# Sharing the block moves of every tile pair between two engines, with fewer and larger transfers in a new order

## Chip, cores and metric

One core of one Trainium2 chip. The metric is the device time of one execution in microseconds (us); the span of a profile is from the first to the last instruction and is some 1.7 us shorter.

## The reference

```python
batch, m, k, n = 16, 512, 1024, 768
# x (16, 512, 1024), weight (1024, 768), add_value (16, 512, 768), all float32; scale = 0.1
return (scale * np.matmul(x, weight) + add_value).astype(np.float32)
```

The 8192 rows of x are 64 tiles of 128 rows. 87 MB move through the core: x 33.6, weight 3.1, add_value 25.2, result 25.2.

## The kernel before

All transfers are issued by SyncE, in the order of a list: x, weight (w), add (a), out (o), each with first tile and number of tiles. Sixteen slots hold x tiles, thirty-two hold add tiles, in which the result is also formed. The weight is staged in add slots 24 to 31.

```python
STREAM = [
    ("x", 0, 3), ("w", 0, 2), ("w", 2, 2), ("w", 4, 2), ("x", 3, 1), ("w", 6, 2),
    ("a", 0, 3), ("x", 4, 4), ("a", 3, 1), ("a", 4, 4), ("x", 8, 4), ("x", 12, 4),
    ("x", 16, 4), ("a", 8, 8), ("x", 20, 4), ("x", 24, 8), ("o", 0, 8), ("a", 16, 8),
    ("x", 32, 8), ("a", 24, 8), ("a", 32, 8), ("x", 40, 8), ("o", 8, 8), ("x", 48, 8),
    # ... cut
    ("a", 56, 8), ("o", 40, 8), ("o", 48, 8), ("o", 56, 4), ("o", 60, 1), ("o", 61, 1),
    ("o", 62, 1), ("l", 63, 1), ("r", 63, 1),          # l, r: the two column parts of one tile
]
X_SLOTS = 16; A_SLOTS = 32; XB_BUFS = 3
MOVED_ACT = [14, 18, 22, ..., 58]      # pairs moved by ScalarE
MOVED_POOL = [16, 20, 24, ..., 56]     # pairs moved by GpSimd
```

TensorE needs x transposed and in bf16. Tiles 0 to 13 and 60 to 63 are cast and transposed by TensorE. The pairs of tiles between are transposed without it: sixteen copies of 32 partitions each cast the pair and rearrange its blocks (the moves), then VectorE turns 32x32 blocks in one instruction. A pair of x slots is free for the next load once it has been moved.

```python
va_pool = tc.tile_pool(name="va_pool", bufs=2)     # pairs moved by ScalarE
vp_pool = tc.tile_pool(name="vp_pool", bufs=2)     # pairs moved by GpSimd

def move_pair(t0, a):                               # called for a = 0..3
    act = t0 in MOVED_ACT
    ...                                             # a == 0: a buffer from va_pool or vp_pool
    for b in range(4):
        move = nc.scalar.copy if act else nc.gpsimd.tensor_copy
        move(moved[t0][32*b:32*b+32, :, a, :], src[32*a:32*a+32, :, b, :])

def step():                                         # one tile
    for j in range(KJ):
        if j == KJ // 2:
            if t + 1 not in in_pair: transpose(t + 1)
            cast_to(min(t + AHEAD, done["x"] - 1))
            for a in range(4):
                if in_pair.get(t + 8 - a) == t + 8 - a: move_pair(t + 8 - a, a)
        product(t, j, BOTH)                         # 512 and 256 columns, bf16
    finish(t, BOTH[0], 0, N)                        # VectorE: scale * product + add, in place
    if in_pair.get(t + 4) == t + 4: turn_moved(t + 4)
```

VectorE runs in program order, so the turn of pair t + 4 comes after the finish of tile t, which may have to wait for its add tile.

Of the kernel before, what the change touches and what calls it, by code (L numbers as in the profile page):

```python
# [9 lines left out]


STREAM = [
    ("x", 0, 3), ("w", 0, 2), ("w", 2, 2), ("w", 4, 2), ("x", 3, 1), ("w", 6, 2),
    ("a", 0, 3), ("x", 4, 4), ("a", 3, 1), ("a", 4, 4), ("x", 8, 4), ("x", 12, 4),
    ("x", 16, 4), ("a", 8, 8), ("x", 20, 4), ("x", 24, 8), ("o", 0, 8), ("a", 16, 8),
    ("x", 32, 8), ("a", 24, 8), ("a", 32, 8), ("x", 40, 8), ("o", 8, 8), ("x", 48, 8),
    ("a", 40, 8), ("o", 16, 8), ("x", 56, 8), ("a", 48, 8), ("o", 24, 8), ("o", 32, 8),
    ("a", 56, 8), ("o", 40, 8), ("o", 48, 8), ("o", 56, 4), ("o", 60, 1), ("o", 61, 1),
    ("o", 62, 1), ("l", 63, 1), ("r", 63, 1),
]  # L20

X_SLOTS = 16
# [3 lines left out]
EARLY = 3  # L26



MOVED_ACT = [14, 18, 22, 26, 30, 34, 38, 42, 46, 50, 54, 58]  # L30
MOVED_POOL = [16, 20, 24, 28, 32, 36, 40, 44, 48, 52, 56]


@with_exitstack
def kernel(
# [8 lines left out]
    nc = tc.nc  # L44
    P = 128
    bf16 = mybir.dt.bfloat16
# [9 lines left out]
    KC = K // (2 * P)  # L56
# [8 lines left out]
    def rows(view, s, n):  # L65
        assert s // G == (s + n - 1) // G
        return view[:, s // G, s % G:s % G + n, :]


    w_v = weight.rearrange("(c p r) n -> p c r n", p=P, r=2)  # L70

    const = ctx.enter_context(tc.tile_pool(name="const", bufs=1))
    xb_pool = ctx.enter_context(tc.tile_pool(name="xb_pool", bufs=XB_BUFS))
    xt_pool = ctx.enter_context(tc.tile_pool(name="xt_pool", bufs=3))
    va_pool = ctx.enter_context(tc.tile_pool(name="va_pool", bufs=2))
    vp_pool = ctx.enter_context(tc.tile_pool(name="vp_pool", bufs=2))
    tp_pool = ctx.enter_context(
        tc.tile_pool(name="tp_pool", bufs=2, space=bass.MemoryType.PSUM))
    mm_pool = ctx.enter_context(
# [6 lines left out]
    ao = const.tile([P, A_SLOTS, N], fp32, name="ao")  # L86
    w_bf = const.tile([P, KJ, N], bf16, name="w_bf")

    xb_tiles, xt_tiles, mm_tiles, done = {}, {}, {}, {"cast": 0, "step": 0, "x": 0}
    in_pair = {t0 + i: t0 for t0 in MOVED_ACT + MOVED_POOL for i in range(2)}  # L90
    moved, cast_pairs = {}, set()

    def load_w(j, n):

        s = A_SLOTS - KJ + j
        if n == 1:
            nc.sync.dma_start(ao[:, s, :], w_v[:, j // 2, j % 2, :])
        else:
            nc.sync.dma_start(ao[:, s:s + 2, :], w_v[:, j // 2, :, :])  # L99
        for i in range(n):  # L100
            nc.vector.tensor_copy(w_bf[:, j + i, :], ao[:, s + i, :])  # L101

    def move_pair(t0, a):


        act = t0 in MOVED_ACT
        if a == 0:
            if act:
                va = va_pool.tile([P, 2 * KC, 4, 64], bf16, tag="va")
            else:  # L110
                va = vp_pool.tile([P, 2 * KC, 4, 64], bf16, tag="vp")
            moved[t0] = va
        k = t0 % X_SLOTS
        assert k + 1 < X_SLOTS
        src = xs[:, k:k + 2, :].rearrange("p i (c b k) -> p (i c) b k", b=4, k=64)
        for b in range(4):
            move = nc.scalar.copy if act else nc.gpsimd.tensor_copy
            move(moved[t0][32 * b:32 * b + 32, :, a, :], src[32 * a:32 * a + 32, :, b, :])  # L118
        if a == 3:
            cast_pairs.add(t0)  # L120

    def turn_moved(t0):
        xt = xt_pool.tile([P, 2, KC, P], fp32, tag="xt")
        for i in range(2):
            xt_tiles[t0 + i] = xt[:, i, :, :]
        nc.vector.transpose(  # L126
            xt.rearrange("p i c m -> p (i c m)"),
            moved.pop(t0).bitcast(fp32).rearrange("p c a k -> p (c a k)"))

    def cast_to(t):  # L130
        while done["cast"] <= t:
            i = done["cast"]
            if i in in_pair:
                assert in_pair[i] in cast_pairs
                done["cast"] += 1
                continue
            if len(xb_tiles) == XB_BUFS:
                break
            xb = xb_pool.tile([P, K], bf16, tag="xb")
            src = xs[:, i % X_SLOTS, :]  # L140
            if i < EARLY:
                nc.vector.tensor_copy(xb[:, 0:K // 2], src[:, 0:K // 2])  # L142
                other = nc.gpsimd.tensor_copy if i else nc.scalar.copy
                other(xb[:, K // 2:K], src[:, K // 2:K])  # L144
            else:
                nc.gpsimd.tensor_copy(xb, src)  # L146
            xb_tiles[i] = xb
            done["cast"] += 1

    def transpose(t, pieces=1):  # L150
        cast_to(t)

        pairs = xb_tiles.pop(t).bitcast(fp32)
        tp = tp_pool.tile([P, KC, P], fp32, tag="tp")
        for c in range(KC):
            nc.tensor.transpose(tp[:, c, :], pairs[:, c * P:(c + 1) * P], identity)  # L156
        if t % 2 == 0:
            xt = xt_pool.tile([P, 2, KC, P], fp32, tag="xt")
            for i in range(2):
                xt_tiles[t + i] = xt[:, i, :, :]  # L160
        q = KC // pieces
        evacuate = nc.scalar.copy if t <= EARLY or t > LAST_PAIR else nc.vector.tensor_copy
        for c in range(0, KC, q):
            evacuate(  # L164
                xt_tiles[t][:, c:c + q, :].bitcast(bf16), tp[:, c:c + q, :].bitcast(bf16))
# [5 lines left out]
    def product(t, j, cols):  # L171
        if (t, cols[0]) not in mm_tiles:
            mm = mm_pool.tile([P, 1024], fp32, tag="mm")
            for part in cols:
                mm_tiles[t, part] = mm
        for n0, n1 in cols:
            nc.tensor.matmul(  # L177
                mm_tiles[t, cols[0]][:, n0:n1], lhs(t, j), w_bf[:, j, n0:n1],
                start=(j == 0), stop=(j == KJ - 1))
# [3 lines left out]
    def finish(t, part, n0, n1):  # L183
        a = ao[:, t % A_SLOTS, n0:n1]
        nc.vector.scalar_tensor_tensor(  # L185
            a, mm_tiles[t, part][:, n0:n1], float(scale), a,
            op0=mybir.AluOpType.mult, op1=mybir.AluOpType.add)
# [27 lines left out]
                        op0=mybir.AluOpType.mult)  # L215
            done["step"] = EARLY

    LAST_PAIR = max(in_pair)
    EARLY_AT = A_SLOTS - KJ - EARLY

    def step():
        t = done["step"]
        if t < T - 1:
            for j in range(KJ):
                if j == KJ // 2:
                    if t + 1 not in in_pair:
                        transpose(t + 1)
                    cast_to(min(t + AHEAD, done["x"] - 1))
                    for a in range(4):
                        if in_pair.get(t + 8 - a) == t + 8 - a:  # L230
                            move_pair(t + 8 - a, a)
                product(t, j, BOTH)
            finish(t, BOTH[0], 0, N)
            if in_pair.get(t + 4) == t + 4:
                turn_moved(t + 4)
        else:
            for cols in BOTH:
                for j in range(KJ):
                    product(t, j, [cols])
                finish(t, cols, *cols)  # L240
        done["step"] += 1

    def added(t):
        assert done["step"] >= EARLY
        nc.vector.tensor_add(  # L245
            ao[:, t, :], ao[:, EARLY_AT + t, :], ao[:, t, :])

    for op, s, n in STREAM:
        last = s + n - 1
        if op == "w":  # L250
            load_w(s, n)
            head(op, s, n)
        elif op == "x":
            if last >= X_SLOTS:
                while done["cast"] <= last - X_SLOTS:
                    step()
            k = s % X_SLOTS
            nc.sync.dma_start(xs[:, k:k + n, :], rows(x_v, s, n))  # L258
            done["x"] = s + n
            if last < EARLY:  # L260
                head(op, s, n)
        elif op == "a":
            k = s % A_SLOTS
            nc.sync.dma_start(ao[:, k:k + n, :], rows(add_v, s, n))  # L264
            for t in range(s, min(s + n, EARLY)):
                added(t)
        else:
            while done["step"] <= last:
                step()
            k = s % A_SLOTS  # L270
            n0, n1 = {"o": (0, N), "l": (0, CUT), "r": (CUT, N)}[op]
            nc.sync.dma_start(rows(out_v, s, n)[:, :, n0:n1], ao[:, k:k + n, n0:n1])  # L272
# [35 lines left out]
```

## Time and profile before

| | before |
|---|---|
| time, median (lowest to highest), us | 210.12 (210.09 to 210.5) |
| data queue: packets, share of 16 engines' span | 5616, 98.2% |
| busy: TensorE, VectorE, ScalarE, GpSimd | 87%, 49%, 62%, 60% |

The share of the queue, the time for which the 16 DMA engines are busy with its packets, is what to read first. Here are the moves, from the costliest groups of the kernel before (partitions x elements, count, then busy us and mean ns of one, then idle time before them):

```profile
L118 ACT CAST va<-xs 32x512 bf16<-32x512 f32 x192 | 118.2, 616 | 28.8 <-DMA xs<-in_x_dram 19.1
L118 POOL CAST va<-xs 32x512 bf16<-32x512 f32 x176 | 106.8, 607 | 15.9 <-DVE xt L126 6.2
```

A pair is sixteen of them on one engine, about 10 us, with the two engines working on different pairs side by side.

### The profile page before, as it was taken

What the parts mean: (1) busy time and instruction counts of PE and PEld (TensorE: products, weight loads), DVE (VectorE), ACT (ScalarE), POOL (GpSimd) and SP (SyncE); (2) the same over time, 40 slices, a digit from 0 to 9 for tenths busy, and PEclk for the clock granted to TensorE, in tenths of its full rate; (3) what the DMA queues carried; (4) which work ended last, traced back from release to release, by engine and by line L of the source; (5) the groups of instructions that cost most, each with busy time, mean ns of one, the idle gap of its engine ahead of it and who ended that gap; (6) DMA issues with size and microseconds to landing.
All of it is one profiled execution on the core that took longest, in us unless ns stands there. A gap on an engine that the chain in (4) does not pass through costs nothing.

```text
span 208.5 us, 2886 instructions
## 1 busy us (share of the span) xinstructions
PE 181.6 (87%) x1096; PEld 110.7 (53%) x1096; DVE 101.3 (49%) x111; ACT 129.0 (62%) x206; POOL 124.3 (60%) x199
## 2 busy tenths in 40 slices
PE   0599399980899997999999999999999999989960
PEld 0455256650466664566666666666666666656630
DVE  0536535511466514855655555555553685233330
ACT  2423000499959798599999999999999900003210
POOL 1310524379898980999998899999999960001000
PEclk9999889996589999999999999999999999999997
DMA  6999999999999999999999999999999999999995
GB/s 236 415 428 440 413 429 434 421 450 406 454 418 448 407 429 462 404 443 420 442 434 413 461 418 424 420 429 437 421 434 424 432 439 424 429 418 439 429 394 214
DMA packets 5629, 87.21 MB, mean 418 GB/s; under 512 B 624, under 2 KB 752, under 8 KB 2032
## 3 DMA queue, kind: packets, MB, share of 16 engines
q1 hardware_dynamic: 5616, 87.03, 98.2%
q8 instruction: 8, 0.13, 0.3%
q14 instruction: 5, 0.04, 0.0%
HBM read 61.87 MB, written 25.17 MB: 417 GB/s over the span
## 4 chain that ended last, share of the span: by engine, by line
DMA 75%; ACT 9%; PE 7%; DVE 3%; SPq 1%; issue 1%; DVEq 0%
DMA out_dram<-ao 35%; DMA ao<-in_add_value_dram 22%; DMA xs<-in_x_dram 13%; ACT va L118 9%; PE mm L177 6%; DMA ao<-in_weight_dram 5%; DVE ao L185 2%; DVE xt L126 1%; PE tp L156 1%; SPq L258 1%; SPq L99 0%; SPq L264 0%; SPq L272 0%; DVEq L185 0%
## 5 line engine op out<-in xcount | busy, mean ns | idle before, releaser
L177 PE MATMUL mm<-w_bf,xt 128*128 128x256 bf16 (+1 forms) x1024 | 173.8, 331 | 8.8 <-DVE xt L164 6.6
L177 PEld LDWEIGHTS <-xt 128*128 128x128 bf16 x1024 | 101.3, 99 | 76.9 <-DVE xt L164 7.0
L118 ACT CAST va<-xs 32x512 bf16<-32x512 f32 x192 | 118.2, 616 | 28.8 <-DMA xs<-in_x_dram 19.1
L118 POOL CAST va<-xs 32x512 bf16<-32x512 f32 x176 | 106.8, 607 | 15.9 <-DVE xt L126 6.2
L185 DVE SCALAR_TENSOR_TENSOR ao<-mm,ao 128x768 f32<-128x768 f32 (+2 forms) x62 | 58.1, 942 | 78.1 <-PE mm L177 49.1
L146 POOL CAST xb<-xs 128x1024 bf16<-128x1024 f32 x15 | 15.2, 1040 | 43.4 <-PE tp L156 22.5
L164 ACT COPY xt<-tp 128x512 bf16<-128x512 bf16 (+1 forms) x11 | 8.2, 785 | 35.3 <-PE tp L156 35.3
L126 DVE STREAM_TRANSPOSE xt<-va 128x1024 f32<-128x1024 f32 x23 | 28.4, 1234 | 0.0
L156 PE MATMUL tp<-identity,xb 128*128 128x128 f32 x72 | 12.9, 314 | 11.2 <-DVE xb L142 7.4
L156 PEld LDWEIGHTS tp<-identity,xb 128*128 128x128 f32 x72 | 9.8, 161 | 13.7 <-issue 7.6
L164 DVE COPY xt<-tp 128x1024 bf16<-128x1024 bf16 x10 | 6.9, 686 | 10.1 <-PE tp L156 10.1
L101 DVE CAST w_bf<-ao 128x768 bf16<-128x768 f32 x8 | 4.1, 556 | 3.8 <-DMA ao<-in_weight_dram 3.8
L142 DVE CAST xb<-xs 128x512 bf16<-128x512 f32 x3 | 1.9, 696 | 6.8 <-DMA xs<-in_x_dram 6.8
L144 POOL CAST xb<-xs 128x512 bf16<-128x512 f32 x2 | 1.6, 834 | 5.5 <-DMA xs<-in_x_dram 5.5
L144 ACT CAST xb<-xs 128x512 bf16<-128x512 f32 x1 | 0.6, 618 | 4.8 <-DMA xs<-in_x_dram 4.8
L213 DVE TENSOR_SCALAR ao<-mm 128x768 f32<-128x768 f32 x2 | 1.8, 952 | 1.9 <-PE mm L177 1.9
L245 DVE TENSOR_TENSOR ao<-ao 128x768 f32<-128x768 f32 x3 | 2.7, 951 | 0.0
L144 ACT ACT_TABLE_LOAD x1 | 1.3, 1283 | 0.7 <-PEq L289 0.7
L210 ACT ACTIVATE ao<-mm 128x768 f32<-128x768 f32 x1 | 0.8, 817 | 0.0
masks.py:197 POOL MEMSET identity<- 128x128 f32 x1 | 0.2, 204 | 0.3 <-POOLq L289 0.3
masks.py:199 POOL TENSOR_SCALAR_AFFINE_SELECT identity<-identity 128x128 f32<-128x128 f32 x1 | 0.3, 292 | 0.1
L289 POOL MEMSET const-float32-0.0<- 128x1 f32 x1 | 0.1, 98 | 0.2 <-issue 0.2
(3 smaller groups left out, 0.3 us busy)
## 6 DMA issues: line engine op xcount, KB each, us to landing
ao<-in_add_value_dram SPq DMA_DIRECT2D x7, 3072.0 KB, 26.1
out_dram<-ao SPq DMA_DIRECT2D x7, 3072.0 KB, 23.9
xs<-in_x_dram SPq DMA_DIRECT2D x5, 4096.0 KB, 18.8
xs<-in_x_dram SPq DMA_DIRECT2D x5, 2048.0 KB, 26.6
ao<-in_weight_dram SPq DMA_DIRECT2D x4, 768.0 KB, 9.6
xs<-in_x_dram SPq DMA_DIRECT2D x1, 1536.0 KB, 6.1
ao<-in_add_value_dram SPq DMA_DIRECT2D x1, 1536.0 KB, 19.3
out_dram<-ao SPq DMA_DIRECT2D x1, 1536.0 KB, 12.9
```

What stands on the lines that cost most here:

```text
L101: nc.vector.tensor_copy(w_bf[:, j + i, :], ao[:, s + i, :])
L118: move(moved[t0][32 * b:32 * b + 32, :, a, :], src[32 * a:32 * a + 32, :, b, :])
L126: nc.vector.transpose(xt.rearrange("p i c m -> p (i c m)"), moved.pop(t0).bitcast(fp32).rearrange("p c a k -> p (c a k)"))
L142: nc.vector.tensor_copy(xb[:, 0:K // 2], src[:, 0:K // 2])
L144: other(xb[:, K // 2:K], src[:, K // 2:K])
L146: nc.gpsimd.tensor_copy(xb, src)
L156: nc.tensor.transpose(tp[:, c, :], pairs[:, c * P:(c + 1) * P], identity)
L164: evacuate(xt_tiles[t][:, c:c + q, :].bitcast(bf16), tp[:, c:c + q, :].bitcast(bf16))
L177: nc.tensor.matmul(mm_tiles[t, cols[0]][:, n0:n1], lhs(t, j), w_bf[:, j, n0:n1], start=(j == 0), stop=(j == KJ - 1))
L185: nc.vector.scalar_tensor_tensor(a, mm_tiles[t, part][:, n0:n1], float(scale), a, op0=mybir.AluOpType.mult, op1=mybir.AluOpType.add)
L245: nc.vector.tensor_add(ao[:, t, :], ao[:, EARLY_AT + t, :], ao[:, t, :])
L258: nc.sync.dma_start(xs[:, k:k + n, :], rows(x_v, s, n))
```

## The change

The intent: both engines work on every pair, so that a pair is ready in half the time; the transfers are larger, 28 in place of 39, and ordered so that each can be issued long before its turn. The core of the diff:

```diff
 STREAM = [
-    ("x", 0, 3), ("w", 0, 2), ("w", 2, 2), ("w", 4, 2), ("x", 3, 1), ("w", 6, 2),
-    ...
-    ("o", 62, 1), ("l", 63, 1), ("r", 63, 1),
+    ("x", 0, 4), ("w", 0, 4), ("w", 4, 4), ("a", 0, 8), ("x", 4, 4), ("x", 8, 8),
+    ("a", 8, 8), ("x", 16, 8), ("a", 16, 8), ("a", 24, 8), ("x", 24, 8), ("o", 0, 8),
+    ("o", 8, 8), ("x", 32, 8), ("a", 32, 8), ("x", 40, 8), ("o", 16, 8), ("a", 40, 8),
+    ("x", 48, 8), ("a", 48, 8), ("o", 24, 8), ("x", 56, 8), ("o", 32, 8), ("a", 56, 8),
+    ("o", 40, 8), ("o", 48, 8), ("o", 56, 5), ("o", 61, 3),
 ]
-MOVED_ACT = [14, 18, ...]; MOVED_POOL = [16, 20, ...]
+MOVED = [14, 16, 18, ..., 58, 60, 62]
-    vp_pool = tc.tile_pool(name="vp_pool", bufs=2)
-def move_pair(t0, a):
+def move_pair(t0, half):
         for b in range(4):
-            move = nc.scalar.copy if act else nc.gpsimd.tensor_copy
-            move(...a...)
+            for a, move in ((2 * half, nc.scalar.copy), (2 * half + 1, nc.gpsimd.tensor_copy)):
+                move(...a...)
-                    for a in range(4):
-                        if in_pair.get(t + 8 - a) == t + 8 - a: move_pair(t + 8 - a, a)
+                    for half in range(2):
+                        if in_pair.get(t + 6 - half) == t + 6 - half: move_pair(t + 6 - half, half)
```

The loading of the weight is changed to take four parts in one transfer, and tiles 60 to 63 are moved too and no longer transposed by TensorE. One of two pools is gone: two buffers for moved pairs in all, where there were four. The moves of a pair start six tiles ahead of their use and no longer eight.

## The prediction

> **What bounds the kernel now.** I read the page first for the share of each engine and of the transfers.
>
> ```profile
> span 208.5 us, 2886 instructions
> PE 181.6 (87%) x1096; PEld 110.7 (53%) x1096; DVE 101.3 (49%) x111; ACT 129.0 (62%) x206; POOL 124.3 (60%) x199
> ...
> PEclk9999889996589999999999999999999999999997
> DMA  6999999999999999999999999999999999999995
> ...
> q1 hardware_dynamic: 5616, 87.03, 98.2%
> ```
>
> The row of tenths for DMA is 9 in all slices but the first and the last, and the one queue that moves data is busy for 98.2% of 16 engines' span, 204.7 us of 208.5. No compute engine is near that, so the kernel is bound by transfers in every stage. I then asked for fixed stretches of the span, to see whether a stage hides a gap:
>
> ```profile
> 20.00:25.00 5.00, 1.53 (x10) 0.88 (x9) 3.00 (x4) 0.00 (x0) 1.57 (x2) 0.97 1.01 422
> ...
> 40.00:60.00 20.00, 13.43 (x69) 7.94 (x68) 5.70 (x8) 18.77 (x31) 15.57 (x25) 0.74 1.00 429
> ...
> 200.00:205.00 5.00, 1.58 (x12) 0.88 (x9) 1.12 (x2) 0.00 (x0) 0.00 (x0) 1.00 0.98 402
> ```
>
> Columns: stretch, length, busy us of PE, PEld, DVE, ACT, POOL, granted clock, DMA share, GB/s. TensorE idles for 3.5 us of the first stretch and 6.6 us of the second, and the DMA share stays at 1.0: compute idles for lack of data, and it costs nothing. Third, the queue's own waits, because the chain of waits cannot show how far ahead a transfer was issued (it names "ACT va L118" and "PE mm L177" beside DMA although the DMA engines were full):
>
> ```profile
> SPq L258 <- ACT va L118: 90.1, 5, 22.0
> SPq L264 <- DMA out_dram<-ao: 40.1, 4, 23.2
> SPq L272 <- DVE ao L185: 21.7, 8, 6.9
> SPq L258 <- DMA xs<-in_x_dram: 14.7, 3, 7.4
> ```
>
> SyncE waits long, but for issues that are tens of us ahead of their turn. The last line shows a second limit: the transfers use eight semaphores in turn, so number n+8 is issued only after number n has landed (number 9 at 6.81 us, when number 1 landed at 0.74 + 6.1). Eight in flight are some 50 us of work once transfers are large.
>
> The trace also records each packet. Median durations by size: 3072 B 121 ns, 6144 B 234, 9216 B 352, 12288 B 461, 16384 B 614, 24576 B 912, 32768 B 1213, and 9 ns for each 4 B semaphore write. A line through 3072 and 32768 gives 1092 ns for 29696 B, 27.2 B/ns per engine or 435 GB/s for 16, and about 8 ns fixed per packet. The data (x 33.55 MB, weight 3.15, add 25.17, out 25.17: 87.03) takes 200.1 us at that rate.
>
> **What the Trainium skill says.** "DMA: Bandwidth & Descriptors", section Specifications, puts the fabric ceiling at 435 GB/s; the slope above agrees. The same page, section Rules for kernel authors, asks for at least 1 MiB per transfer and for coalescing; alone, a 1 MB transfer is listed there at 78% of peak. This trace does not show that loss: with a full queue the stretch from 190 to 195 us, with 3 MB outputs, has 433 GB/s, and the early stretch from 10 to 15 us, with transfers of 0.5 to 1.2 MB, has 427. What is left of the rule here is 8 ns per packet. "TensorE: Matmul & The Clock Gate", Part 1, says that an idle window of about 3.4 us drops TensorE to half its clock. The trace agrees: it ran at half clock for 3.4 us after the idle 20 to 24.5 us, and for 10.2 us around the idle of 46.4 to 53 us.
>
> **The change part by part.** Bytes stay the same.
>
> Packets: 39 transfers become 28. Before, every transfer has one data packet per partition and 16 semaphore writes: 39 x 144 = 5616, as the page says. After, each weight half carries two 6144 B runs per partition: 28 x 144 + 2 x 128 = 4288. That is 1328 fewer, 83 per engine, at 8 ns: 0.7 us saved. Direct sum as a check, eight packets per engine and transfer, with mean durations (24576 B 917 ns, 32768 B 1220 ns): before 204.1 us, after seven x of 9.76, two x of 4.94, two weight halves of 3.75, eight add and seven out of 7.34, the last outs 4.59 (15360 B, interpolated 574 ns) and 2.82, with 0.14 per transfer already inside: 203.4. Saved again 0.7 us.
>
> Calibration: with 4.2 us for start and landing, this ledger puts the landing of add tiles 8 to 15 at 51.3 us and of add 16 to 23 at 80.8 in the kernel before, and the trace has 51.2 and 80.8. At the end it is 0.7 late (208.3 against 207.6). For the kernel after it gives these landings: weights 12.9 and 16.7; add 0-7 24.0, 8-15 46.1, 16-23 63.2, 24-31 70.5, 32-39 112.1, 40-47 136.6, 48-55 153.7, 56-63 185.5; x 4-7 29.0, 8-15 38.7, 16-23 55.8, 24-31 80.3, 32-39 104.8, 40-47 121.9, 48-55 146.3, 56-63 170.8; out 0-7 87.6, 8-15 95.0, 16-23 129.2, 24-31 161.0, 32-39 178.1, 40-47 192.8, 48-55 200.2, 56-60 204.8, 61-63 207.6.
>
> Start: both kernels begin with an x transfer issued at 0.7 us and data at 1.75 us. Unchanged. The later weights and x tiles 4 to 7 (landing about 29 us, after 23.3) delay TensorE, not the queue.
>
> Moves: before, ACT does 192 of 616 ns and POOL 176 of 607; after, 25 pairs x 8 = 200 each. Started back to back they are 0.626 us apart on ACT and 0.647 on POOL (16 in 10.36 us), so a pair takes 8 x 0.647 = 5.2 us on both, in place of 10 us on one; the throughput is the same two tiles per 5.2 us, the latency half. That beside the queue's 203.4/64 = 3.2 us per tile leaves 18% in hand. TensorE loses four transposes of four pieces, 4 x 0.44 = 1.8 us, off its end. DVE gains two STREAM_TRANSPOSE of 1.23 us. All of it lies beside the transfers, worth nothing directly.
>
> Whether the queue stays fed: I set each issue (the move, finish or landing that frees its slot) against the moment when the transfer ahead of it lands. x 24-31 needs pair 14, about 52 us, against 70.5: 18 ahead. x 32-39 needs pair 22: x 16-23 lands at 55.8, plus four pairs of 5.2 is 76.6, against 95. x 40-47: 80.3 + 20.7 = 101, against 112. x 48-55: 104.8 + 20.7 = 125.5, against 136.6. x 56-63: 125.5 + 20.7 = 146.2, against 161. The add loads wait only for outs that landed 7 to 17 us earlier. Last outs: x 56-63 lands at 170.8, its pairs are moved at 176, 181, 186 and 191.5 and turned 1.2 us later. A step of TensorE is 2.6 us (16 matmuls in the chain), needs its pair turned and the finish of three tiles earlier (three PSUM buffers), and a finish takes 0.95. Finish 55 waits on DVE behind the turn of pair 58 (182.4), so is done at 183.4; finish 56 waits for add 56-63 and is done at 186.5; step 59 then ends at 189.1, 60 at 191.7, 61 at 194.3, 62 at 196.9, 63 at 199.5. So out 56-60 is issued at about 195 against 200.2, and out 61-63 at 200.3 against 204.8. Smallest lead 4.5 us. The queue is never empty.
>
> Sum: 210.12 - 0.7 = 209.4; I add 0.2 for a lead in the tail that may fail. 209.6.
>
> **The rivals.** (1) The tail takes over. In DVE's order the turn of pair 58 stands before the finish of tile 55, and the turn waits for moves of x that landed late, so the last steps bunch. TensorE idles about 4.7 us before tile 56 by my count; if that brings half clock for 3.4 us, the wait for add 56-63 absorbs it; if for 10 us, the end moves to 204 and about 1 us of queue time is lost, with a first-packet delay of 1 us (0.74 to 1.75 us at the start) on top: 210.5 to 212. For it: half clock after both long idles before. Against it: before, the tail had four more transposes and still kept DMA at 0.98 up to 205 us.
> (2) A middle wait empties the queue: POOL's moves, slowed by DVE's work on shared memory, or the two engines each waiting for the other's half. It would take a loss of 11 us in one x block: four pairs of 8 us in place of 5.2. The trace has one POOL span with 80 moves in 52.04 us, 0.65 each, beside a busy DVE. That speaks against it; 213 or more if so.
> (3) A large gain: fewer, larger transfers run nearer the peak. Even at no cost per packet, 200.1 + 4 us of start and landing + 1.6 us between span and measured time gives 205.7, which is barely 2% under; with 8 ns per packet it is out of reach.
>
> **Range and chances.** The gain is bounded by packets (0.7 us, perhaps 1.0 with the engines' uneven tail), the loss by leads of 4.5 us at the end and 11 us before. So 208.8 to 211.5 should hold eight times in ten. Two per cent is 4.2 us: faster than 205.9 lies at the ceiling, chance 0.02; slower than 214.3 needs an empty queue for 5 us, chance 0.04; within 0.94.
>
> **What would show it.** Right: data-queue packets 4288, its busy time near 204 us of a span of about 207.8, no DMA slice under 9 but the first and last, moves still about 0.62 us and 200 on each engine, no SyncE wait ending after its predecessor landed. TensorE may idle more in the first 30 us, and early slices of granted clock may drop, without cost. Wrong: a slice of DMA at 8 or less in the middle (rival 2, with the name of the wait in the queue's own list), or in the last three slices with out 61-63 issued after 205 us (rival 1), or packets of the same size with longer durations, which nothing here foresees.

## The result and the profile after

The changed kernel took 210.09 us (210.04 to 210.34, four runs) against 210.28 for the kernel before in the same rounds. The ratio was 0.9993, with a 95% interval of 0.9976 to 1.001: the same.

The head of the page of the kernel after (busy time, share and instructions by engine; granted clock and DMA share in tenths over 40 slices; the data queue):

```profile
span 208.6 us, 2840 instructions
PE 178.8 (86%) x1059; PEld 108.9 (52%) x1080; DVE 102.1 (49%) x113; ACT 129.9 (62%) x210; POOL 135.2 (65%) x219
...
PEclk9999979999999999999999799999999999999995
DMA  6999999999999999999999999999999999999994
...
q1 hardware_dynamic: 4288, 87.03, 97.8%
```

The DMA row is as full as before. There are 4288 packets instead of 5616 and 97.8% of 208.56 us is 204.0 us of queue time, 0.7 less than before, yet the span has not shrunk: 208.6. The stretches that answer to those shown of before:

```profile
40.00:60.00 20.00, 19.84 (x130) 13.11 (x132) 11.87 (x15) 7.76 (x14) 13.74 (x21) 1.00 0.99 426
...
200.00:205.00 5.00, 0.00 (x0) 0.00 (x0) 0.34 (x1) 0.00 (x0) 0.00 (x0) 0.77 0.94 399
```

From 40 to 60 us TensorE is now busy throughout where it idled 6.6 us before, and the bytes moved are the same (426 against 429 GB/s). This is the plainest sign that compute does not set the pace. After 200 us TensorE has nothing left, where it was still working before. The moves, from the groups, and the wait that leads VectorE's list:

```profile
L110 ACT CAST va<-xs 32x512 bf16<-32x512 f32 x200 | 123.2, 616 | 45.1 <-DMA xs<-in_x_dram 42.6
L110 POOL CAST va<-xs 32x512 bf16<-32x512 f32 x200 | 121.7, 608 | 21.6 <-DMA xs<-in_x_dram 12.7
```
```profile
DVE xt L119 <- POOL va L110: 54.6, 23, 5.6
```

Each move costs what it did. Both engines now wait for x above all, and VectorE waits for nearly every pair (23 times). The queue's own waits:

```profile
SPq L250 <- ACT va L110: 67.8, 5, 22.1
SPq L264 <- DVE ao L178: 49.2, 5, 21.2
SPq L256 <- DMA out_dram<-ao: 27.1, 3, 13.1
```

SyncE still waits long, but no wait outlasts what is queued: by the trace, every transfer is issued at least 1.6 us before the first of the 16 engines is done with the transfer ahead of it. Last, the end: VectorE's last finish in the kernel before, then in the kernel after:

```profile
201.62 0.42 DVE L185 SCALAR_TENSOR_TENSOR ao<-mm,ao 128x256 f32<-128x256 f32 x1 [0.18 <-PE mm L177]
```
```profile
199.92 0.42 DVE L178 SCALAR_TENSOR_TENSOR ao<-mm,ao 128x256 f32<-128x256 f32 x1 [0.18 <-PE mm L170]
```

Compute ends 1.7 us earlier, and the last landing hardly moves: 207.6 before, 207.5 after.

The trace also records when each of the 16 engines has landed its share of a transfer. For the last transfer, the first engine is done at 205.2 us before and 204.7 after, the last engine at 207.6 and 207.5. So the saved packets are seen at the first engine (0.5 us), and hardly at the last, which ends the kernel.

### The profile page after: what moved, and what is told of

The parts are those of the page before. It is cut to its first block, busy times and chain, and to the rows that moved or that the text cites. A ratio compares the mean times of both kernels' runs of the same rounds, so it can differ in the third digit from the quotient of the medians. Undisturbed runs are those within 1.5% of the kernel's fastest.

```text
span 208.6 us, 2840 instructions
## 1 busy us (share of the span) xinstructions
PE 178.8 (86%) x1059; PEld 108.9 (52%) x1080; DVE 102.1 (49%) x113; ACT 129.9 (62%) x210; POOL 135.2 (65%) x219
## 3 DMA queue, kind: packets, MB, share of 16 engines
q1 hardware_dynamic: 4288, 87.03, 97.8%
## 4 chain that ended last, share of the span: by engine, by line
DMA 65%; PE 15%; POOL 13%; issue 1%; SPq 1%; DVE 1%; POOLq 0%; DVEq 0%
DMA out_dram<-ao 28%; DMA xs<-in_x_dram 25%; PE mm L170 13%; DMA ao<-in_add_value_dram 12%; POOL va L110 12%; PE tp L149 2%; POOL xb L139 2%; DVE ao L178 1%; SPq L256 0%; SPq L93 0%; SPq L250 0%; POOLq L139 0%; DVEq L178 0%; SPq L264 0%; POOLq L110 0%
## 5 line engine op out<-in xcount | busy, mean ns | idle before, releaser
L170 PE MATMUL mm<-w_bf,xt 128*128 128x512 bf16 (+1 forms) x1003 | 172.1, 330 | 7.0 <-DVE ao L178 5.1
L110 ACT CAST va<-xs 32x512 bf16<-32x512 f32 x200 | 123.2, 616 | 45.1 <-DMA xs<-in_x_dram 42.6
L110 POOL CAST va<-xs 32x512 bf16<-32x512 f32 x200 | 121.7, 608 | 21.6 <-DMA xs<-in_x_dram 12.7
L178 DVE SCALAR_TENSOR_TENSOR ao<-mm,ao 128x768 f32<-128x768 f32 (+2 forms) x62 | 55.8, 924 | 17.7 <-PE mm L170 15.5
L119 DVE STREAM_TRANSPOSE xt<-va 128x1024 f32<-128x1024 f32 x25 | 31.1, 1245 | 54.6 <-POOL va L110 54.6
L139 POOL CAST xb<-xs 128x1024 bf16<-128x1024 f32 x11 | 11.2, 1042 | 27.7 <-DMA xs<-in_x_dram 24.2
L149 PE MATMUL tp<-identity,xb 128*128 128x128 f32 x56 | 10.2, 317 | 14.0 <-DVE xb L135 8.6
L149 PEld LDWEIGHTS tp<-identity,xb 128*128 128x128 f32 x56 | 7.7, 163 | 16.0 <-issue 8.6
L157 DVE COPY xt<-tp 128x1024 bf16<-128x1024 bf16 x10 | 6.9, 688 | 10.5 <-PE tp L149 10.5
L157 ACT COPY xt<-tp 128x512 bf16<-128x512 bf16 (+1 forms) x7 | 4.1, 655 | 9.3 <-PE tp L149 9.3
```

The lines of the kernel that those rows point to most:

```text
L110: move(moved[t0][32 * b:32 * b + 32, :, a, :], src[32 * a:32 * a + 32, :, b, :])
L119: nc.vector.transpose(xt.rearrange("p i c m -> p (i c m)"), moved.pop(t0).bitcast(fp32).rearrange("p c a k -> p (c a k)"))
L139: nc.gpsimd.tensor_copy(xb, src)
L149: nc.tensor.transpose(tp[:, c, :], pairs[:, c * P:(c + 1) * P], identity)
L157: evacuate(xt_tiles[t][:, c:c + q, :].bitcast(bf16), tp[:, c:c + q, :].bitcast(bf16))
L170: nc.tensor.matmul(mm_tiles[t, cols[0]][:, n0:n1], lhs(t, j), w_bf[:, j, n0:n1], start=(j == 0), stop=(j == KJ - 1))
```

## The experiments

Twelve kernels ran.

### The moves alone: new moves, old order

```diff
 # the changed kernel with
-STREAM = [... 28 transfers]
+STREAM = [... the 39 of before]
```

> The moves shared by both engines, with the old 39 transfers. Theory (the queue is always full, so only packets and the slowest of the 16 engines count): 5616 packets, 204.7 us of queue busy, ratio 0.998 to 1.002 to the kernel before. Rival (the halved latency of a pair is itself worth or costs something): over 0.5% either way, with a slice of DMA under 9 in the middle.

Measured: 218.15 us, ratio 1.0379 (1.0364 to 1.0395), slower by 8 us. The theory failed. Two stretches of this kernel, then the same two of the kernel before:

```profile
100.00:108.00 8.00, 8.00 (x51) 4.86 (x50) 4.12 (x4) 7.85 (x13) 7.46 (x13) 1.00 0.85 329
120.00:130.00 10.00, 10.00 (x64) 6.01 (x62) 5.91 (x6) 9.79 (x17) 9.33 (x16) 1.00 0.79 317
```
```profile
100.00:108.00 8.00, 8.00 (x51) 4.87 (x50) 4.03 (x5) 7.84 (x14) 7.46 (x13) 1.00 1.02 436
120.00:130.00 10.00, 10.00 (x64) 5.99 (x63) 5.73 (x7) 9.80 (x17) 9.29 (x17) 1.00 0.98 421
```

The DMA share falls to 0.85 and 0.79: the queue runs dry, though every compute engine is as busy as before. What came late is seen further up in this kernel's timelines of VectorE, ScalarE, GpSimd and SyncE:

```profile
80.86 0.96 DVE L180 SCALAR_TENSOR_TENSOR ao<-mm,ao 128x768 f32<-128x768 f32 x1 [7.27 <-DMA ao<-in_add_value_dram]
```
```profile
83.00 60.39 ACT L112 CAST va<-xs 32x512 bf16<-32x512 f32 x96 [5.82 <-DVE xt L121]
```
```profile
83.03 62.64 POOL L112 CAST va<-xs 32x512 bf16<-32x512 f32 x96 [5.64 <-DVE xt L121]
```
```profile
103.90 0.33 SPq L252 DMA_DIRECT2D xs<-in_x_dram  x1
```

VectorE waits 7.3 us for add tiles 16 to 23, and the turns behind that finish wait with it. Both buffers are then full of moved pairs, so both engines stop for 5.6 to 5.8 us. From 83 us on they run without a gap at 5.2 us a pair, and four pairs (24 to 30) bring the issue of x tiles 40 to 47 to 83 + 4 x 5.2 = 103.8 us, where the kernel before had it at 96.0. This became a new theory: two buffers in place of four.

### The same with four buffers

```diff
 # the kernel of the last experiment with
-va_pool = tc.tile_pool(name="va_pool", bufs=2)
+va_pool = tc.tile_pool(name="va_pool", bufs=4)
```

> The shared moves in the old order of 39 transfers, which took 218.15 us, now with four buffers for moved pairs in place of two. Theory (while VectorE waits for an add transfer it turns no pair, so with two buffers the moves stop and x tiles are freed late; the old moves had two buffers per engine, four in all): the queue no longer runs dry at 104 and 124 us, the x transfer after next is issued near 96 us as in the kernel before, 209.8 to 211.5 us. Rival (the sharing itself, or the later place of the moves in the program, makes the x tiles free late): stays over 215 us.

Measured: 210.14 us, ratio 1.0005 (0.9992 to 1.0018). The issue of the same x transfer, and the two stretches:

```profile
93.40 0.33 SPq L252 DMA_DIRECT2D xs<-in_x_dram  x1
```
```profile
100.00:108.00 8.00, 8.00 (x51) 4.79 (x50) 4.02 (x4) 7.85 (x13) 7.46 (x13) 1.00 1.01 435
120.00:130.00 10.00, 10.00 (x64) 6.04 (x62) 5.73 (x7) 9.79 (x17) 9.27 (x17) 1.00 0.99 426
```

The transfer is issued 10.5 us earlier, which is two pairs of 5.2 us: just what two more buffers let the engines do while VectorE waits. The whole loss of 8 us is gone. So sharing the moves costs nothing, and the loss was the halved number of buffers. The new order does not need them: its add tiles 16 to 23 have landed by 63 us, before VectorE asks for them.

### The order alone: old moves, 28 transfers

```diff
 # the kernel before with
+STREAM = [... the 28 transfers], and the loading of the weight and the start that go with them
```

> The 28 transfers in the new order, with the old moves (a pair wholly on one engine) and the four transposes at the end. Theory: 4288 packets, 204.0 us of queue busy, ratio 0.996 to 1.000; the last finish comes about 1.8 us later than with the new moves (202 us against 200.3) and still ahead of the 204.7 at which the transfer before lands, so nothing is lost. Rival (the new order needs the new moves to be fed): out 61-63 is issued after 204.7 us, or an x load after its turn, and the time is over 211.

Measured: 213.74 us, ratio 1.018 (1.0159 to 1.0202). I expected a last finish at 202 us; it came at 207.6. Two stretches of this kernel, then the same two of the changed kernel:

```profile
190.00:200.00 10.00, 10.00 (x68) 6.41 (x66) 3.67 (x4) 2.02 (x2) 1.04 (x1) 1.00 0.76 327
200.00:210.00 10.00, 7.15 (x46) 4.16 (x44) 3.03 (x4) 2.02 (x2) 0.00 (x0) 0.98 0.64 269
```
```profile
190.00:200.00 10.00, 9.83 (x61) 5.75 (x59) 5.54 (x7) 1.05 (x2) 1.77 (x3) 1.00 0.99 426
200.00:210.00 10.00, 0.00 (x0) 0.00 (x0) 0.34 (x1) 0.00 (x0) 0.00 (x0) 0.63 0.54 230
```

The queue is dry for a quarter of the stretch before 200 us and again after 205. The cause lies at the last x block, which lands at 170.5 us here: VectorE's turn of its first pair waits for a whole-pair move, first in this kernel, then in the changed one:

```profile
181.02 1.25 DVE L124 STREAM_TRANSPOSE xt<-va 128x1024 f32<-128x1024 f32 x1 [7.74 <-POOL va L116]
```
```profile
176.20 1.25 DVE L119 STREAM_TRANSPOSE xt<-va 128x1024 f32<-128x1024 f32 x1 [5.13 <-POOL va L110]
```

That is 4.8 us later. With the four transposes of 0.44 us that only this kernel has in its tail (1.8 us) it is 6.6 of the 7.3 us by which the last finish is late. TensorE also ran at half clock from 182.4 to 185.8 us, which may be the rest. My expectation had counted the 1.8 and forgotten the first. Two more runs took the two causes one at a time.

### Transposes in the tail

```diff
 # the changed kernel with
-MOVED = [14, ..., 58, 60, 62]
+MOVED = [14, ..., 58]                              # 60 to 63 by TensorE, evacuated by ScalarE
```

> The changed kernel, but the last four tiles are transposed by TensorE as before and not moved. Theory: the last finish comes 4 x 0.44 = 1.8 us later, 202.1 us, still ahead of 204.7, so the time stays within 0.3% of 210.1. Rival (these transposes were what made the new order with the old moves slow): 212 us or more.

Measured: 210.16 us (209.84 to 211.09), ratio 1.0002 (0.9989 to 1.0015). The last finish begins at 202.39 us, so it is 2.5 us later, not 1.8, in a profile in which the add transfer before it also landed 0.7 us later (186.3 against 185.6). The time is the same within the stated 0.3%; the changed kernel's own ratio was 0.9992, so some 0.1% may be lost. The profiled run was the slowest of the six (211.09 us), and its trace shows how thin the lead is: out 61-63 is issued 0.9 us after the first engine is done with the transfer ahead and 2.6 us before the last engine is. The first engine runs dry, yet the last landing (208.2 us) is only 0.7 us later than in the first profile of the changed kernel: the last engine still had work.

### A whole pair per engine in the last block only

```diff
 # the changed kernel with, in move_pair
+                if t0 in (56, 58):
+                    move = nc.scalar.copy if t0 == 58 else nc.gpsimd.tensor_copy
```

> The changed kernel, but pairs 56 and 58, the first two of the last x block, are moved wholly by one engine each (10 us side by side instead of 5.2 us one after the other). Theory (in the last block the latency of the first pair is on the path): the turn of pair 56 comes 5 us later, at 182.3, the last finish at 204 to 205.5, out 61-63 is issued after the transfer before it has ended on most engines, and the time is 211 to 212.7. Rival (only the rate of the moves counts): within 0.3% of 210.1.

Measured: 214.14 us, ratio 1.0197 (1.0182 to 1.0212). The direction holds, the size was too small: the last finish begins at 206.55 us, not by 205.5. TensorE's timeline and the granted clock of this run show what was missing:

```profile
183.54 22.98 PE L172 MATMUL mm<-w_bf,xt 128*128 128x512 bf16 x128 [6.60 <-DVE ao L180]
```
```profile
PEclk9999957999999999999996999999999999589999
```

TensorE idles for 6.6 us: the finish that it waits for stands in VectorE's order behind the turn of the late pair (181.4 us). Its clock is halved from 180.8 to 187.7 us, so the first tiles of the last block also run slowly. This is the first rival of the prediction, brought about on purpose. In the changed kernel the wait before tile 56 is 1.4 us and the clock stays full there.

### The last eight tiles in one transfer

```diff
-    ("o", 56, 5), ("o", 61, 3),
+    ("o", 56, 8),
```

> The last eight tiles leave in one transfer of 3 MB instead of five and three tiles. Theory (my count of leads: last finish at 200.3, queue dry at about 200.2 at its slowest engine and 197.4 at its fastest): the transfer is issued at 200.7, its data begins 1.0 us later, takes 7.34 us and the landing is at 209.2 to 210.5, so the time is 211.5 to 213. Rival (a lead in the tail is not needed, the slowest engine hides it): within 0.5 us of 210.1.

Measured: 211.71 us (211.18 to 212.99), ratio 1.0081 (1.0056 to 1.0106). It is issued at 200.0 us (200.7 was expected), 2.8 us after the first engine and 0.2 us after the last is done with the transfer ahead, and the profiled run shows the gap:

```profile
190.00:200.00 10.00, 9.46 (x59) 5.46 (x56) 5.89 (x7) 0.82 (x2) 1.52 (x3) 1.00 0.78 334
```

The cut into five and three tiles is worth 1.6 us; the counts of leads in the tail hold.

### Many small packets

```diff
-x_v = x_f.rearrange("(g p t) k -> p g t k", p=P, t=G)      # and add, out alike
+x_v = x_f.rearrange("(g t p) k -> p g t k", p=P, t=G)
```

> The same 28 transfers, order and result, but each partition takes rows that lie apart in memory, so that a transfer of 8 tiles has 1024 data packets of 3 or 4 KB instead of 128 of 24 or 32 KB: 25536 packets in place of 4288, 1328 more per engine. Theory (8 ns a packet): 10.6 us longer, 220 to 221.5 us. Rival 1 (packets cost nothing beside the bytes): within 1 us of 210.1. Rival 2 (rows that lie apart also cost in memory): over 223.

Measured: 219.11 us, ratio 1.0419 (1.0403 to 1.0435), correct. The changed kernel took 210.08, so 1328 more packets per engine (by chance the number that the change saves on all 16 together) cost 9.0 us, 6.8 ns each. That is below the 8 ns that the packets' durations gave and far from nothing. For the 83 packets per engine that the change saves it makes, by estimate, 0.56 us in place of 0.7.

### The changed kernel again

> The changed kernel unaltered, for a tighter interval and a second trace. Theory: ratio to before 0.998 to 1.000 (the packets saved 0.7 us per engine on average, but the slowest engine's end moved by only 0.1 us). If the whole 0.7 us shows in some runs: 0.997.

Measured: 210.08 us (209.78 to 210.66), ratio 0.9992 (0.9978 to 1.0006). Both put the gain at 0.15 to 0.17 us. Both intervals include no gain at all and end at 0.5 us at most. In this second profile the span is 208.1, the first engine is done at 204.5 us and the last at 207.0.

### Does TensorE's own program hold the last engine back?

The traces show a second queue beside the data: 16 KB pieces of program, fetched eight times in a run some 20 us apart, each about 1.05 us on one engine. After the first of them (30.3 us before, 35.7 after) one engine alone lands its share 1.7 to 1.9 us after the first engine, and the other fifteen still land within 0.4. I took this for the reason why the slowest engine gained nothing, and made TensorE's program shorter, with wrong results on purpose:

```diff
 def product(t, j, cols):
+    if j not in (0, 2, 5, KJ - 1): return      # half of the products
```
```diff
+    if j: return                               # one of eight (and stop=True)
```
```diff
+    if j: return                               # one of eight, and only the first 512 columns
```

> Wrong result on purpose: four of eight products, 1038 rows for TensorE, transfers unchanged. Theory: 4 fetches, spread at the end 1.6 to 2.5 us, the time 0.3 to 1.2 us under the whole kernel's 210.1. Rival 1: spread and time unchanged within 0.3 us.

> Wrong result on purpose: only the first of eight products of each tile, so TensorE's program has 270 rows instead of 2062, all transfers unchanged. Theory (each 16 KB piece of program is fetched through one of the 16 engines and sets its share of the data back by about 1.4 us; the end waits for the engine that is furthest behind): fetches fall from 8 to 1, the spread between first and last engine at the end from 2.8 us to 0.4 to 1.6, the end comes 1.0 to 2.0 us earlier, 208.1 to 209.1 us. Rival 1 (the spread comes from uneven engines or from slow packets): spread stays over 2 us and the time within 0.3 us of 210.1. Rival 2 (TensorE's work bounds something after all): the time falls by more than 3 us.

> Wrong result on purpose: one matmul of 512 columns per tile, so TensorE's program has 142 rows, and with it no piece of program has to be fetched during the run (the run with 270 rows had one fetch, at 55.6 us, and its slowest engine was 3.2 us behind at the end). Theory (a single fetch is enough to make one engine the last): no fetch, spread at the end 0.8 to 1.7 us, last landing 205.4 to 206.5, time 208.4 to 209.6. Rival (the slow packets that hit all engines near 77 and 166 us make one engine last): spread over 2 us, time 210 to 210.8.

As a control, full program but short matmuls:

```diff
         for n0, n1 in cols:
+            n1 = n1 if j in (0, KJ - 1) else n0 + 128
```

> Wrong result on purpose: products 1 to 6 of each tile with 128 columns instead of 512 and 256. The same number of TensorE instructions, but each step much shorter (about 1.9 us instead of 2.6, by my estimate). Control for the runs with fewer products. Theory of the fetches: 8 fetches, spread at the end 2.2 to 2.9 us, the time within 0.3 us of the unaltered 210.1. Rival (fewer products helped because compute was shorter): faster by as much as the run with half the products.

| kernel | fetches | last transfer landed: first engine, last engine, us | mean of the 16 engines behind the first, us | time, us | ratio |
|---|---|---|---|---|---|
| before | 8 | 205.2, 207.6 | 1.24 | 210.12 | 1 |
| after | 8 | 204.7, 207.5 | 1.41 | 210.09 | 0.9993 |
| after, again | 8 | 204.5, 207.0 | 1.39 | 210.08 | 0.9992 |
| short matmuls | 8 | 204.7, 206.9 | 1.30 | 210.04 | 0.9987 |
| half of the products | 4 | 204.6, 207.7 | 0.98 | 210.63 | 1.002 |
| one of eight | 1 | 204.6, 207.8 | 0.76 | 210.79 | 1.003 |
| one of eight, 512 columns | 1 | 204.6, 207.0 | 0.63 | 210.18 | 1.0011 |

The theory falls. The fetches are real and set the average engine back (1.2 to 1.4 us with eight, 0.6 to 0.8 with one), but the last engine ends at 206.9 to 207.8 whatever their number, and the kernels with a short program are not faster. The run meant to have no fetch still had one. That run also has the five 8 KB pieces of a third queue (most take 0.31 us), which every kernel here has; after the first of them, at 59.4 us, one engine lands 0.8 us behind the first in place of 0.3, still before the fetch at 90.4 us. My explanation is that an engine that is hit once, and again by some of the slow packets that the traces of the new order show at about 77 us and in some runs at 167 us, on several engines at once, is enough to be last; no run here shows it, since the landings do not name their engine. Why the kernels with half and an eighth of the products come out 0.2 to 0.3% slower than the kernel before I cannot say. The control shows that shorter matmuls alone change nothing that the noise lets one see.

## Why the prediction was right

**What bounds it.** Right. The queue is full in both kernels (98.2 and 97.8%), TensorE's work can be cut to one eighth with no gain, and the 6.6 us that TensorE no longer idles at 46 to 53 us bought nothing.

**The ledger of landings** (when each transfer was said to have landed). Right to 0.7 us from 38 us on: x 24 to 31 at 80.3 against 81.0 measured, x 56 to 63 at 170.8 against 170.9, the last landing at 207.6 against 207.5. The four landings before that came 1.1 to 1.3 us earlier than said (add 0-7 at 22.8, not 24.0): probably because the 4.2 us for start and landing were fitted to later transfers, when one engine was already behind (after the first piece of program, see the last experiment). The packets are as worked out (4288). The direct sum of durations was 0.6 us low in both kernels (204.1 and 203.4 against 204.7 and 204.0), and right in the difference.

**The leads** (how long before the transfer ahead has landed each one is issued). The issue times were right where the end depends on them: out 61-63 was to be issued at 200.3 us and SyncE's last issue ended at 200.7. Merging the last two transfers cost what this count said. But the smallest lead, 4.5 us, was counted to the last engine's landing. Measured it is 4.4 us there and only 1.6 us at the first engine, of which some 1.0 us passes before the first packet moves. The tail was closer to running dry than the prediction said.

**The packets' 0.7 us.** In the queue's own busy time the saving is there (204.7 to 204.0 us). In the kernel's time the size was too large, and even the sign is not clear of the noise: the term "1328 fewer, 83 per engine, at 8 ns: 0.7 us saved" measured 0.15 to 0.17 us. Two parts of this are shown: the cost per packet on the whole kernel's time is 6.8 ns, which makes 0.56; and the saving is there at the first engine (0.5 to 0.6 us earlier), while the last engine, 2.4 to 2.8 us behind, moved by 0.1 in one profile and 0.6 in the other. The run with the old order and four buffers is a second trace of 39 transfers and ends as the kernel before does (205.1 and 207.6 us). What decides which engine is last, and by how much, stays open. My sum treated the 16 engines as one.

**The moves.** "the throughput is the same two tiles per 5.2 us, the latency half ... worth nothing directly" is right for the whole change and hides most of what is in it. The new order with the old moves loses 3.6 us, because the latency of the first pair of the last block is then on the path; the new moves with the old order lose 8 us. The prediction did not look at the buffers: the change also takes two of four away, and of the two orders only the new one, with its earlier add transfers, makes that harmless. A prediction for either half of this change by the same steps would have been wrong, and my expectations for both runs were.

**Rival 1.** It did not happen, because the idle time before tile 56 was 1.4 us and not the 4.7 that I counted; TensorE was behind my count (tile 55 ended at 176.9 us), probably held to the pairs' pace, since VectorE waited for 23 of 25 pairs. Made to happen by whole-pair moves, it cost 4.1 us. **Rivals 2 and 3** did not happen; the run of the moves alone shows what rival 2 looks like, though with buffers and not rates as the cause.

**Two readings** in the prediction are loose. TensorE's first long idle time before the change ran from 21.0 us, not 20, to 24.5. And the 78% for 1 MB, quoted from "DMA: Bandwidth & Descriptors", stands there in a table of transfers issued by GpSimd. The transfers here are issued by SyncE, so this trace is no test of that figure.

## What to carry to other kernels

When the transfer queue is full from start to end, a change of compute or of order can only keep it full: ask of each part when its transfer is issued and what is still queued then, and count the buffers that let engines run on while another waits. Two parts of a change that look independent can each need the other; run them singly before crediting either. Count to the first of the 16 engines when asking whether the queue runs dry, and to the last when asking when the kernel ends: here they were 2.4 to 2.8 us apart, and 0.7 us saved in the queue's time was at most 0.5 us in the kernel's.

## What the Trainium skill lacked or had wrong

- "DMA: Bandwidth & Descriptors", Rules for kernel authors: the advice of at least 1 MiB per transfer and of coalescing does not say how little it brings where the queue is already full. Here 39 transfers, some of 0.1 to 0.8 MB, became 28, and the time fell by 0.16 us of 210, which is within the noise.
- The same page, section "Why small descriptors are slow (HBM only)", gives a fixed overhead per packet in cycles for small descriptors. It has no figure for packets of some KB. On 3 and 4 KB packets the runs show 6.8 ns per packet and engine in the whole time (25536 packets against 4288: 9.0 us); the line through the packets' durations gave 8 ns.
- "Perfetto Trace Analysis", section What "DMA-bound" means, names single DMA engines as what can bind; this agrees (the last engine lands 2.2 to 3.2 us after the first in the kernels of the table).
- "Runtime: NRT & Kernel Launch", section Instruction fetch mechanics, says that a program is refilled in blocks of 16 KiB through a DMA queue of its own, and calls the cost mostly hidden. The traces agree on the blocks (eight of 16 KB). What the page lacks is that a block delays data: each takes 1.05 us on one of the 16 engines, and after the first one that engine lands some 1.4 us later than it did.
- "TensorE: Matmul & The Clock Gate", Part 1, puts the half clock after an idle window of about 3.4 us. These profiles show that shorter idle times can do it and longer ones need not: it followed 2.5 us of idle (110.5 to 113.0 us, transposes in the tail), 2.6 us (90.6 to 93.2 us, the order alone) and 3.1 us (109.6 to 112.7 us, the changed kernel), but not 3.2 us (109.4 to 112.6 us) in the second profile of the changed kernel.
